# Closing seven-block products: where raw weight chunks lie, how far ahead they are loaded, and where VectorE's sums stand

## The chip, the cores and the metric

The kernel runs on one core of one Trainium2 chip. The metric is device time in microseconds (us), the median of the timed executions. TensorE is called PE, VectorE DVE, ScalarE ACT, GpSimd POOL and SyncE SP, as in the profile; PEld is PE's loading of weights.

## The reference, cut to what matters

An encoder of two layers over 512 tokens of width 1024, in float32. Each layer has an attention part and then a squared-ReLU MLP:

```python
def sq_relu_mlp(h, w_up, w_down):
    u = jax.nn.relu(h @ w_up)
    return (u * u) @ w_down
...
        h = h + sq_relu_mlp(rmsnorm(h, norm_ffn[layer]), ffn_w_up[layer], ffn_w_down[layer])
```

`w_up` is 1024 x 4096 and `w_down` 4096 x 1024. The change concerns a part of `h = h + (u * u) @ w_down` in each of the two layers.

## The kernel before

**Split products.** A float32 product is made of three matmuls: each operand is split into a high half rounded to a shorter format and a low half that holds the rest (high x high, high x low, low x high). For weights, ACT writes the high half (tile `whi`, three buffers) and DVE subtracts it from the raw weights to give the low half (`wlo`, four buffers).

**The down product.** In `mlp` the 32 row blocks of `w_down` are used in three manners: six and, at the end, two (layer 0) or four (layer 1) by plain products, eight by `product8`, and 16 or 14 by `Seven`, a Strassen-like scheme: of a 2 x 2 arrangement of blocks it makes seven products instead of eight, at the price of sums of blocks. I call the `Seven` product of the down matrix the closing product. It has four output blocks m = 0 to 3 (256 columns each), and each takes `np` chunks: 8 in layer 0, 7 in layer 1. So there are 32 and 28 chunks, numbered on from 0 here. A chunk is 21 matmuls of 128x256 on PE (L459 to L461, three for each of seven products).

**A chunk's way** (`seven_chunk`): SP loads two rows of 256 columns (256 KB, L360); three sums of its 128x128 blocks follow (L365, L366, L367), on POOL or, for two chunks (kp 2 and 5) of the output blocks m = 1 to 3, on DVE; ACT makes the high half of all seven blocks in one instruction of 896 columns (L371), DVE the low half (L372). The raw chunk lies in a tile `raw` (four buffers) or in a free slot `a` when more slots are free than `reserve`.

**An output block's end** (`Seven.run` and `evac` in `mlp`): ACT copies one PSUM half (L467), DVE adds the others (L468 to L471) and then adds 128x1024 into `hT` (L1600). `product8` before it ends in eight DVE additions into `hT` (L1556).

**What sets the order.** The program is written in PE's order. `weights(i)` is called for each chunk before its matmuls; it asks for loads up to `LOAD` = 5 chunks ahead, begins the sums of what is loaded, and makes high and low halves two chunks ahead. A scheduler then places each engine's instructions, except where `tc.keep_in_program_order` holds them: POOL's sums are held, DVE's are not. Each engine works its row in order, and SP's queue likewise: an instruction that waits holds what stands behind it.

**Other tiles that the change uses.** `scratch()` gives 128x512 tiles `sc` (six buffers), used for temporary results throughout; `spare_p` gives 128x512 tiles `p` (five buffers), the attention's probability tiles, used in the MLP for the last two operands of `product8`.

Of the kernel before, what the change touches and what calls it, by code (L numbers as in the profile page):

```python
# [8 lines left out]
F32 = mybir.dt.float32  # L9
F32R = mybir.dt.float32r  # L10
I32 = mybir.dt.int32
AF = mybir.ActivationFunctionType
ALU = mybir.AluOpType
# [3 lines left out]
S = 512  # L17
D = 1024
P = 128
# [11 lines left out]
def f32(ap):  # L31
    return ap.bitcast(F32)
# [3 lines left out]
def encoder_kernel(ctx: ExitStack, tc: tile.TileContext, ins, out, dbg=None):  # L36
    nc = tc.nc
    PE, ACT, DVE, POOL, SP = nc.tensor, nc.scalar, nc.vector, nc.gpsimd, nc.sync
# [3 lines left out]
    wp = ctx.enter_context(tc.tile_pool(name="wp", bufs=3))  # L42
# [19 lines left out]
    def nm(s):  # L62
        cnt[0] += 1
        return f"{s}_{cnt[0]}"
# [206 lines left out]
    def rows(w, k0, nk):  # L271
        return w[k0 * P : (k0 + nk) * P, :].rearrange("(k p) n -> p k n", p=P)


    asked, loaded, ready, low_parts = [], [], [], []
    AHEAD, SUM, LOAD = 2, 3, 5
    begun = [0]

    def plan(*spec, make=None, **more):
        asked.append((make or chunk, spec, more))  # L280
        return len(asked) - 1
# [7 lines left out]
    def begin(i):  # L289
        while begun[0] < len(loaded):  # L290
            make = asked[begun[0]][0]
            if make is summed_chunk and begun[0] > i + SUM:
                break
            if make in (summed_chunk, seven_chunk):
                next(loaded[begun[0]])
            begun[0] += 1

    def weights(i, ahead=AHEAD):
        while len(loaded) < min(i + LOAD + 1, len(asked)):
            preload(len(loaded) + 1)  # L300
            begin(i)
        begin(i)
        while len(ready) < min(i + ahead + 1, len(asked)):
            hi, lo, lows = next(loaded[len(ready)])
            ready.append((hi, lo))
            low_parts.append(lows)

            give_low(len(ready) - fixed[0])
        give_low(i + 1)
        return ready[i]  # L310
# [38 lines left out]

    SEVEN = [(0, 0), (2, 2), (4, 5), (3, 3), (5, 4), (6, 1), (1, 6)]

    reserve = [3]
    def seven_chunk(w, k0, c0, eng=None):


        slot = Slot(F32) if len(free) > reserve[0] else None
        raw = slot.t if slot else wp.tile([P, 1024], F32, tag="raw", bufs=4, name=nm("raw"))
        SP.dma_start(raw[:, 0:512].rearrange("p (k n) -> p k n", k=2), rows(w, k0, 2)[:, :, c0 : c0 + 256])  # L360
        r = raw.rearrange("p (b n) -> p b n", n=P)
        yield
        held = (lambda z: z) if eng else tc.keep_in_program_order
        eng = eng or POOL
        held(eng.tensor_tensor(r[:, 6], r[:, 0], r[:, 1], op=ALU.subtract))  # L365
        held(eng.tensor_tensor(r[:, 4:6], r[:, 2:3].to_broadcast([P, 2, P]), r[:, 0:7:6], op=ALU.add))  # L366
        held(eng.tensor_tensor(r[:, 7], r[:, 3], r[:, 5], op=ALU.subtract))  # L367
        yield
        hi = wp.tile([P, WIDE], F32R, tag="whi", name=nm("whi"))[:, 16:912]
        lo = wp.tile([P, WIDE], F32R, tag="wlo", bufs=4, name=nm("wlo"))[:, 48:944]  # L370
        ACT.activation(hi, raw[:, 128:1024], AF.Copy)  # L371
        DVE.tensor_tensor(lo, raw[:, 128:1024], f32(hi), op=ALU.subtract)  # L372
        if slot:
            slot.free()
        yield hi, lo, []

    class Seven:
# [60 lines left out]
            for s_ in self.slots.values():  # L438
                s_.free()

        def plan(self, w, c0, pairs=None):

            return [plan(w, pairs[kp] if pairs else 2 * kp, c0, DVE if pairs and c0 and kp in (2, 5) else None,
                         make=seven_chunk)
                    for kp in range(self.np)]

        def run(self, ids, evac):
# [1079 lines left out]
    def mlp(l, last=None, then=lambda: None):  # L1527

        stage, ahead, later = first_product(l)
        reserve[0] = 3
        w = ins["ffn_w_down"][l]
        up4, gens4 = [], []

        def plain_last(k0, V):
            left = list(V)
            gens4.extend(product(w, k0, up4, tiles(512 * c, 512), lambda j, b, c=c: ev(4 * c + j, b), nk=2 * len(V))
                         for c in range(2))  # L1540

            def beside(m, i):
                if m == 2 and i % 8 == 4 and left:
                    w_ = left.pop(0)
                    for z in range(2):
                        U4.append(Slot())
                        up4.append(U4[-1].pair())
                        split(w_.t[:, S * z : S * z + S], up4[-1])
                    w_.free()

            return beside

        U4 = []

        def ev(m, b):
            return DVE.tensor_tensor(hT[:, m, :], hT[:, m, :], b, op=ALU.add)  # L1556

        U, _, _, (at_u, _), _ = stage(SIZES[l][0])
        up = [s_.pair() for s_ in U]
        gens = [product(w, at_u, up, tiles(512 * c, 512), lambda j, b, c=c: ev(4 * c + j, b)) for c in range(2)]  # L1560
        ahead()
        for c, gen in enumerate(gens):
            for i, _ in enumerate(gen):
                later(c, i)
        for s_ in U:
            s_.free()
        ids8 = []
        U, R, V, (at_u, at_r), late = stage(*SIZES[l][1:], lambda at: ids8.extend(
            plan8(w, [k + z for k in at for z in range(2)])))
        gen = product8(ids8, U, ev)  # L1570
        u7 = Seven(2 * len(R))
        ids = [u7.plan(w, 256 * m, at_r) for m in range(4)]
        k0 = 32 - 2 * len(V)
        beside = (last or plain_last)(k0, V)
        then()
        bias = iter(()) if last else bias_rows()
        reserve[0] = NSLOT
        work, at = convert(u7, R), 0
        for _ in range(10):
            next(work)  # L1580
        for i, _ in enumerate(gen):
            if i in (1, 4, 6):
                next(late, None)
            next(bias, None)

            at += 9 * len(R) + 2
            while at > 0:
                next(work, None)
                at -= 8 * len(U) - 2
        for x in (work, bias):  # L1590
            for _ in x:
                pass
        reserve[0] = 3 if last else 2
        for m in range(4):
            if m == 1 and not last:
                hold["tables"].free()

            def evac(w_):
                h2 = hT[:, 2 * m : 2 * m + 2, :]
                DVE.tensor_tensor(h2, h2, w_.t.rearrange("p (z n) -> p z n", z=2), op=ALU.add)  # L1600

            for i, _ in enumerate(u7.run(ids[m], evac)):
                beside(m, i)
        u7.free()
        for gen in gens4:
            for _ in gen:
                pass
        for s_ in U4:
            s_.free()
# [530 lines left out]
```

## Time and profile before

| | |
|---|---|
| median of 3 timed runs | 1134.73 us (1134.01 to 1135.53) |
| the profiled execution | 1136.11 us, its span 1134.3 us |
| granted TensorE clock | 0.998 over the span |
| closing products | about 486 to 564 us and 1032 to 1101 us |
| ACT making high halves of raw chunks (L371) | 55.2 us in 58 instructions |
| DVE making low halves of raw chunks (L372) | 69.7 us in 58 instructions |

How to read the rows of the profile: a group has line, engine, operation, output<-input by tile, shape and count, then busy time and mean ns, then the idle time before it and what ended that. A row of the timeline has start, duration, engine, line and tiles, and in brackets the idle time before it and what released it. A row of waits says who waited for whom, with total us, times and longest us. A row of windows has the stretch, its length, and busy us with the count of instructions of PE, PEld, DVE, ACT and POOL, then granted clock, DMA share and GB/s.

### The profile page before, as it was taken

How to read it: one execution, taken by the hardware profiler on the slowest of the kernel's cores; microseconds unless marked ns; L12 is line 12 of the kernel's file. 1: busy time of each engine (PE TensorE's matmuls, PEld its weight loads, DVE VectorE, ACT ScalarE, POOL GpSimd, SP SyncE). 2: the span in 40 equal slices, each digit the busy share in tenths (PEclk: the TensorE clock that was granted, in tenths of full speed). 3: DMA queues.
4: the chain of work that ended last, by engine and by line, in shares of the span. 5: the costliest groups of instructions: out<-in, count | busy, mean ns of one | idle time of the engine just before them, and what ended most of it. 6: DMA issues, size and time to landing. Idle time of an engine off the chain costs nothing.

```text
span 1134.3 us, 20502 instructions
## 1 busy us (share of the span) xinstructions
PE 1121.3 (99%) x7348; PEld 1007.5 (89%) x7348; DVE 904.0 (80%) x1571; ACT 667.8 (59%) x1132; POOL 593.3 (52%) x718
## 2 busy tenths in 40 slices
PE   9999999999999999999999999999999999999997
PEld 7787788888899999899998998988889999989996
DVE  7887997978968787979785676667997788798874
ACT  6677785765346668634464555555552676773334
POOL 4366432226788994378522232221287889535640
PEclk9999999999999999999999999999999999999999
DMA  8322442222533334933576574433344223282342
GB/s 241 102 74 77 117 113 70 66 66 75 167 103 91 96 103 121 287 108 103 154 150 166 145 185 125 125 109 123 103 155 132 75 90 99 78 194 69 101 146 75
DMA packets 117237, 135.54 MB, mean 119 GB/s; under 512 B 9859, under 2 KB 98864, under 8 KB 117136
## 3 DMA queue, kind: packets, MB, share of 16 engines
q1 hardware_dynamic: 110736, 119.83, 34.8%
q0 software_dynamic: 6224, 14.31, 6.5%
q8 instruction: 58, 0.95, 0.4%
q14 instruction: 43, 0.35, 0.1%
q10 hardware_dynamic: 176, 0.10, 0.0%
HBM read 112.18 MB, written 6.29 MB: 104 GB/s over the span
## 4 chain that ended last, share of the span: by engine, by line
PE 86%; DVE 5%; issue 4%; POOL 2%; DMA 2%; ACT 1%; SPq 0%; DVEq 0%; POOLq 0%; ACTq 0%
PE mm L618 8%; PE mm L620 8%; PE mm L619 8%; PE mm L461 4%; PE mm L459 4%; PE mm L460 4%; PE s L1143 3%; PE t L461 3%; PE t L459 3%; PE t L460 3%; PE o L1131 3%; PE s L618 2%; PE s L619 2%; PE s L620 2%; PE s L461 2%
## 5 line engine op out<-in xcount | busy, mean ns | idle before, releaser
L618 PE MATMUL mm<-a,whi 128*128 128x512 f32 x428 | 172.7, 404 | 0.1
L372 DVE TENSOR_TENSOR wlo<-a,whi 128x896 fp32r<-128x896 f32 x106 | 135.3, 1282 | 43.8 <-ACT whi L371 43.6
L619 PE MATMUL mm<-a,whi 128*128 128x512 f32 x428 | 167.5, 391 | 0.0
L620 PE MATMUL mm<-a,wlo 128*128 128x512 f32 x428 | 167.2, 392 | 0.0
L371 ACT ACTIVATE whi<-a 128x896 fp32r<-128x896 f32 x106 | 100.9, 952 | 97.3 <-PE s L460 29.0
L226 DVE TENSOR_TENSOR wlo<-raw,whi 128x1024 fp32r<-128x1024 f32 (+3 forms) x94 | 106.8, 1142 | 24.7 <-ACT whi L236 21.8
L236 ACT ACTIVATE whi<-raw 128x1024 fp32r<-128x1024 f32 (+4 forms) x97 | 89.1, 920 | 56.4 <-PE s L619 23.2
L461 PE MATMUL mm<-a,wlo 128*128 128x256 f32 x430 | 119.6, 278 | 0.8 <-DVE wlo L372 0.8
L459 PE MATMUL mm<-a,whi 128*128 128x256 f32 x430 | 118.8, 276 | 0.0
L460 PE MATMUL mm<-a,whi 128*128 128x256 f32 x430 | 118.8, 276 | 0.0
L371 ACT ACTIVATE whi<-raw 128x896 fp32r<-128x896 f32 x58 | 55.2, 956 | 82.7 <-POOL raw L367 22.7
L367 POOL TENSOR_TENSOR a<-a 128x128 f32<-128x128 f32 x104 | 97.8, 940 | 8.2
L366 POOL TENSOR_TENSOR a<-a 128x256 f32<-128x256 f32 x104 | 94.3, 907 | 8.1
L620 PEld LDWEIGHTS mm<-a,wlo 128*128 128x128 f32 x428 | 80.3, 188 | 17.1
L1151 POOL TENSOR_SCALAR p<-p,ti 128x512 f32<-128x512 f32 x64 | 48.0, 750 | 88.6 <-DVE ti L1150 67.8
L618 PEld LDWEIGHTS mm<-a,whi 128*128 128x128 f32 x428 | 80.5, 188 | 15.4 <-issue 0.7
L619 PEld LDWEIGHTS mm<-a,whi 128*128 128x128 f32 x428 | 80.7, 189 | 13.6
L1783 POOL TENSOR_SCALAR p<-p,ti 128x256 f32<-128x256 f32 x64 | 35.6, 567 | 103.4 <-DVE ti L1782 82.4
L459 PE MATMUL t<-a,whi 128*128 128x256 f32 x312 | 86.1, 276 | 0.0
L460 PE MATMUL t<-a,whi 128*128 128x256 f32 x312 | 86.1, 276 | 0.0
L461 PE MATMUL t<-a,wlo 128*128 128x256 f32 x312 | 86.1, 276 | 0.0
L372 DVE TENSOR_TENSOR wlo<-raw,whi 128x896 fp32r<-128x896 f32 x58 | 69.7, 1223 | 19.6 <-ACT whi L371 19.6
(449 smaller groups left out, 3583.1 us busy)
## 6 DMA issues: line engine op xcount, KB each, us to landing
a<-in_ffn_w_up_dram SPq DMA_DIRECT2D x102, 256.0 KB, 2.7
raw<-in_ffn_w_down_dram SPq DMA_DIRECT2D x34, 512.0 KB, 4.3
raw<-in_ffn_w_down_dram SPq DMA_DIRECT2D x56, 256.0 KB, 2.6
raw<-in_od_w_qkv_dram SPq DMA_DIRECT2D x64, 128.0 KB, 3.2
raw<-in_ffn_w_up_dram SPq DMA_DIRECT2D x12, 512.0 KB, 3.8
wlo<-in_ffn_w_down_dram POOLq DMA_DIRECT2D x12, 512.0 KB, 7.5
a<-a SPq DMA_DIRECT2D x17, 256.0 KB, 3.3
bx<-a SPq DMA_DIRECT2D x32, 128.0 KB, 6.1
```

What stands on the lines that cost most here:

```text
L226: z = lambda: (eng or DVE).tensor_tensor(to, src, f32(high), op=ALU.subtract)
L236: ACT.activation(hi[:, 0:m], raw[:, 0:m], AF.Copy)
L366: held(eng.tensor_tensor(r[:, 4:6], r[:, 2:3].to_broadcast([P, 2, P]), r[:, 0:7:6], op=ALU.add))
L367: held(eng.tensor_tensor(r[:, 7], r[:, 3], r[:, 5], op=ALU.subtract))
L371: ACT.activation(hi, raw[:, 128:1024], AF.Copy)
L372: DVE.tensor_tensor(lo, raw[:, 128:1024], f32(hi), op=ALU.subtract)
L459: PE.matmul(o, wh, x[:, 0], start=kp == 0 and n in (0, 1, 3, 5), stop=False, skip_group_check=True)
L460: PE.matmul(o, wh, x[:, 1], start=False, stop=False, skip_group_check=True)
L461: PE.matmul(o, wl, x[:, 0], start=False, stop=kp == self.np - 1, skip_group_check=True)
L618: PE.matmul(o, wh, xh, start=first, stop=False)
L619: PE.matmul(o, wh, xl, start=False, stop=False)
L620: PE.matmul(o, wl, xh, start=False, stop=last)
```

## The change

Three things, all for closing products alone, except that the sums' place within a raw chunk changes for all seven-block chunks (blocks are renumbered in `SEVEN` to match):

1. Of the 32 and 28 chunks, 15 and 11 are loaded into pairs of tiles, either two `sc` or two `p`, by two loads of 128 KB. The first tile holds blocks a0 to a3, the second b0 to b3. Their high and low halves are made in two instructions each, of 384 and 512 columns. The first four chunks and all others stay in `raw` or `a`.
2. `LOAD` is 8 during the closing products, 5 elsewhere.
3. DVE's sums are put off: they are written when PE's chunk is three before theirs, and held in program order.

```diff
-    AHEAD, SUM, LOAD = 2, 3, 5
+    AHEAD, SUM, LOAD = 2, 3, [5]
+    put_off = []
...
             if make in (summed_chunk, seven_chunk):
-                next(loaded[begun[0]])
+                z = next(loaded[begun[0]])
+                if z:
+                    put_off.append((begun[0], z))
             begun[0] += 1
...
     def weights(i, ahead=AHEAD):
-        while len(loaded) < min(i + LOAD + 1, len(asked)):
+        while len(loaded) < min(i + LOAD[0] + 1, len(asked)):
             preload(len(loaded) + 1)
             begin(i)
         begin(i)
+        while put_off and put_off[0][0] <= i + SUM:
+            put_off.pop(0)[1]()
...
-    SEVEN = [(0, 0), (2, 2), (4, 5), (3, 3), (5, 4), (6, 1), (1, 6)]
+    SEVEN = [(0, 0), (4, 2), (6, 5), (5, 3), (1, 4), (2, 1), (3, 6)]
...
-    def seven_chunk(w, k0, c0, eng=None):
-        slot = Slot(F32) if len(free) > reserve[0] else None
-        raw = slot.t if slot else wp.tile([P, 1024], F32, tag="raw", bufs=4, name=nm("raw"))
-        SP.dma_start(raw[:, 0:512].rearrange("p (k n) -> p k n", k=2), rows(w, k0, 2)[:, :, c0 : c0 + 256])
-        r = raw.rearrange("p (b n) -> p b n", n=P)
+    def seven_chunk(w, k0, c0, eng=None, home=None):
+        slot, src = None, rows(w, k0, 2)[:, :, c0 : c0 + 256]
+        if home:
+            parts = [home(F32) for _ in range(2)]
+            for z in range(2):
+                SP.dma_start(parts[z][:, 0:256], src[:, z])
+        else:
+            slot = Slot(F32) if len(free) > reserve[0] else None
+            raw = slot.t if slot else wp.tile([P, 1024], F32, tag="raw", bufs=4, name=nm("raw"))
+            parts = [raw[:, 512 * z : 512 * z + 512] for z in range(2)]
+            SP.dma_start(raw.rearrange("p (k n) -> p k n", k=2)[:, :, 0:256], src)
+        a, b = (t.rearrange("p (b n) -> p b n", n=P) for t in parts)
         yield
-        held = (lambda z: z) if eng else tc.keep_in_program_order
-        eng = eng or POOL
-        held(eng.tensor_tensor(r[:, 6], r[:, 0], r[:, 1], op=ALU.subtract))
-        held(eng.tensor_tensor(r[:, 4:6], r[:, 2:3].to_broadcast([P, 2, P]), r[:, 0:7:6], op=ALU.add))
-        held(eng.tensor_tensor(r[:, 7], r[:, 3], r[:, 5], op=ALU.subtract))
-        yield
+        held = tc.keep_in_program_order
+        later, eng = eng, eng or POOL
+        def sums():
+            held(eng.tensor_tensor(a[:, 2], a[:, 0], a[:, 1], op=ALU.subtract))
+            held(eng.tensor_tensor(b[:, 2:4], b[:, 0:1].to_broadcast([P, 2, P]), a[:, 0:3:2], op=ALU.add))
+            held(eng.tensor_tensor(a[:, 3], b[:, 1], b[:, 3], op=ALU.subtract))
+        if later:
+            yield sums
+        else:
+            sums()
+            yield
...
-        ACT.activation(hi, raw[:, 128:1024], AF.Copy)
-        DVE.tensor_tensor(lo, raw[:, 128:1024], f32(hi), op=ALU.subtract)
+        for to, x in (((0, 384), parts[0][:, P:512]), ((384, 896), parts[1])) if home else (((0, 896), raw[:, P:1024]),):
+            to = slice(*to)
+            ACT.activation(hi[:, to], x, AF.Copy)
+            DVE.tensor_tensor(lo[:, to], x, f32(hi[:, to]), op=ALU.subtract)
...
-        ids = [u7.plan(w, 256 * m, at_r) for m in range(4)]
+        n7, kinds = len(R), dict(R=None, S=scratch, P=spare_p)
+        homes = [kinds["R" if n < 4 else ("RSRSRSR"[n % 7] if last and n > 10 else "RSRPRSRSP"[n % 9])]
+                 for n in range(4 * n7)]
+        ids = [u7.plan(w, 256 * m, at_r, homes[n7 * m : n7 * m + n7]) for m in range(4)]
...
         reserve[0] = 3 if last else 2
+        LOAD[0] = 8
         for m in range(4):
...
+        LOAD[0] = 5
         u7.free()
```

PE's row of instructions is the same in both kernels. On DVE three places matter. The first is the end of `product8` in layer 0, where its eight additions (L1556, in the changed kernel L1577) stand among the first low halves (L372, now L393) of the closing product. Before, with the sums of chunk 13 in tile a_6094:

```order
L1556 TENSOR_TENSOR hT<-hT,t_5415 128x512
L1556 TENSOR_TENSOR hT<-hT,o_5416 128x512
L365 TENSOR_TENSOR a_6094<-a_6094 128x128
L366 TENSOR_TENSOR a_6094<-a_6094 128x256
L1556 TENSOR_TENSOR hT<-hT,mm_5417 128x512
L367 TENSOR_TENSOR a_6094<-a_6094 128x128
L372 TENSOR_TENSOR wlo_5830<-raw_5654,whi_5829 128x896
L1556 TENSOR_TENSOR hT<-hT,mm_5418 128x512
L1556 TENSOR_TENSOR hT<-hT,mm_5419 128x512
L1556 TENSOR_TENSOR hT<-hT,s_5420 128x512
L372 TENSOR_TENSOR wlo_5849<-raw_5716,whi_5848 128x896
```

and now:

```order
L1577 TENSOR_TENSOR hT<-hT,t_5415 128x512
L1577 TENSOR_TENSOR hT<-hT,o_5416 128x512
L1577 TENSOR_TENSOR hT<-hT,mm_5417 128x512
L393 TENSOR_TENSOR wlo_5830<-raw_5654,whi_5829 128x896
L1577 TENSOR_TENSOR hT<-hT,mm_5418 128x512
L1577 TENSOR_TENSOR hT<-hT,mm_5419 128x512
L1577 TENSOR_TENSOR hT<-hT,s_5420 128x512
L393 TENSOR_TENSOR wlo_5870<-raw_5716,whi_5869 128x896
L393 TENSOR_TENSOR wlo_5900<-raw_5765,whi_5899 128x896
```

The three sums have left this place; they now stand behind the low half of chunk 11. The second place is the end of output block 1 in layer 1 on DVE. The low half behind the 1024-wide addition is chunk 17's, and the sums are chunk 19's (raw_12681 before, sc_12676 and sc_12677 now). Before:

```order
L468 TENSOR_TENSOR a_12670<-a_12670,mm_12457 128x2x256
L469 TENSOR_TENSOR a_12670<-a_12670,mm_12458 128x512
L372 TENSOR_TENSOR wlo_12687<-raw_12580,whi_12686 128x896
L470 TENSOR_TENSOR a_12670<-a_12670,mm_12458 128x256
L365 TENSOR_TENSOR raw_12681<-raw_12681 128x128
L471 TENSOR_TENSOR a_12670<-a_12670,s_12459 128x512
L366 TENSOR_TENSOR raw_12681<-raw_12681 128x256
L1600 TENSOR_TENSOR hT<-hT,a_12670 128x1024
L367 TENSOR_TENSOR raw_12681<-raw_12681 128x128
L372 TENSOR_TENSOR wlo_12724<-raw_12610,whi_12723 128x896
```

and now:

```order
L489 TENSOR_TENSOR a_12770<-a_12770,mm_12545 128x2x256
L490 TENSOR_TENSOR a_12770<-a_12770,mm_12546 128x512
L491 TENSOR_TENSOR a_12770<-a_12770,mm_12546 128x256
L393 TENSOR_TENSOR wlo_12789<-raw_12580,whi_12788 128x896
L492 TENSOR_TENSOR a_12770<-a_12770,s_12547 128x512
L1625 TENSOR_TENSOR hT<-hT,a_12770 128x1024
L393 TENSOR_TENSOR wlo_12823<-sc_12609,whi_12822 128x384
L393 TENSOR_TENSOR wlo_12823<-sc_12610,whi_12822 128x512
L379 TENSOR_TENSOR sc_12676<-sc_12676 128x128
L380 TENSOR_TENSOR sc_12677<-sc_12677,sc_12676 128x256
L381 TENSOR_TENSOR sc_12676<-sc_12677 128x128
L393 TENSOR_TENSOR wlo_12860<-raw_12644,whi_12859 128x896
```

The sums have gone from between the additions to behind chunk 17's low half, which is made in two pieces. At the end of block 0 of layer 0 the order of the additions and of the low halves behind them is as before, except that chunk 10's low half comes in two pieces. The third place is SP's queue at the start of layer 1's closing product (chunks 0 to 2 first; a_12227 is chunk 5 before; the loads of the two kernels carry the lines L360 before, and L372 and L367 now). Before:

```order
L360 DMA raw_12012<-in_ffn_w_down_dram 128x2x256
L360 DMA raw_12058<-in_ffn_w_down_dram 128x2x256
L360 DMA raw_12111<-in_ffn_w_down_dram 128x2x256
L360 DMA a_12227<-in_ffn_w_down_dram 128x2x256
L360 DMA raw_12149<-in_ffn_w_down_dram 128x2x256
L360 DMA raw_12161<-in_ffn_w_down_dram 128x2x256
L360 DMA raw_12263<-in_ffn_w_down_dram 128x2x256
L360 DMA raw_12299<-in_ffn_w_down_dram 128x2x256
L360 DMA raw_12329<-in_ffn_w_down_dram 128x2x256
L360 DMA raw_12359<-in_ffn_w_down_dram 128x2x256
```

and now:

```order
L372 DMA raw_12072<-in_ffn_w_down_dram 128x2x256
L372 DMA raw_12118<-in_ffn_w_down_dram 128x2x256
L372 DMA raw_12171<-in_ffn_w_down_dram 128x2x256
L372 DMA a_12294<-in_ffn_w_down_dram 128x2x256
L367 DMA sc_12287<-in_ffn_w_down_dram 128x256
L372 DMA raw_12209<-in_ffn_w_down_dram 128x2x256
L367 DMA sc_12288<-in_ffn_w_down_dram 128x256
L367 DMA sc_12299<-in_ffn_w_down_dram 128x256
L367 DMA sc_12300<-in_ffn_w_down_dram 128x256
L367 DMA sc_12377<-in_ffn_w_down_dram 128x256
L367 DMA sc_12378<-in_ffn_w_down_dram 128x256
L372 DMA raw_12221<-in_ffn_w_down_dram 128x2x256
```

Chunks 5, 7 and 10 (the sc tiles) and 6 (a_12294) now stand ahead of chunk 4's load into a raw buffer (raw_12221), where loads into raw buffers stood.

More of the change, by code (lines that the diff above doesn't have):

```diff
@@ L439, in free, with plan @@
                 s_.free()
-        def plan(self, w, c0, pairs=None):
+        def plan(self, w, c0, pairs=None, homes=None):
             return [plan(w, pairs[kp] if pairs else 2 * kp, c0, DVE if pairs and c0 and kp in (2, 5) else None,
-                         make=seven_chunk)
+                         make=seven_chunk, home=homes[kp] if homes else None)
                     for kp in range(self.np)]
```

## The prediction, made before the changed kernel ran

> **What bounds the kernel now.** I read the page first, then what TensorE (PE) waits for, then the order of time around each wait.
>
> ```profile
> PE 1121.3 (99%) x7348; PEld 1007.5 (89%) x7348; DVE 904.0 (80%) x1571; ACT 667.8 (59%) x1132; POOL 593.3 (52%) x718
> ...
> PE s L461 <- DVE wlo L372: 1.7, 1, 1.7
> PE mm L461 <- DVE wlo L372: 0.8, 1, 0.8
> ```
>
> PE is busy 99% of the span, so a change that leaves its work alone can win only what PE waits. Its two waits for the low halves of seven-block weights (L372) both lie in the closing products. The page counts a pipelined matmul as busy to its modelled end, so I price a stall from start to start:
>
> ```profile
> 491.55 0.28 PE L460 MATMUL s<-a,whi 128*128 128x256 f32 x1
> 491.84 0.39 PE L461 MATMUL s<-a,wlo 128*128 128x256 f32 x1
> 492.06 0.28 PE L459 MATMUL t<-a,whi 128*128 128x256 f32 x1
> ...
> 513.16 0.28 PE L459 MATMUL mm<-a,whi 128*128 128x256 f32 x1
> 513.27 0.28 PE L460 MATMUL mm<-a,whi 128*128 128x256 f32 x1
> 514.30 0.39 PE L461 MATMUL mm<-a,wlo 128*128 128x256 f32 x1 [0.75 <-DVE wlo L372]
> 514.52 0.28 PE L459 MATMUL mm<-a,whi 128*128 128x256 f32 x1
> ...
> 1073.03 0.28 PE L460 MATMUL s<-a,whi 128*128 128x256 f32 x1
> 1074.96 0.39 PE L461 MATMUL s<-a,wlo 128*128 128x256 f32 x1 [1.65 <-DVE wlo L372]
> 1075.18 0.28 PE L459 MATMUL t<-a,whi 128*128 128x256 f32 x1
> ```
>
> These are the records on both sides of the three places where PE's rhythm breaks. The rhythm itself, from the windows (PE busy first, then PEld, DVE, ACT, POOL; some matmul records are missing, so I count from the code):
>
> ```profile
> 392.00:420.00 28.00, 28.00 (x245) 27.75 (x244) 23.56 (x28) 18.68 (x23) 26.36 (x31) 1.00 0.31 95
> 505.69:525.76 20.07, 19.32 (x170) 19.12 (x169) 16.89 (x20) 8.92 (x11) 17.46 (x20) 1.00 0.37 118
> 525.76:544.80 19.04, 19.04 (x170) 19.04 (x169) 17.10 (x19) 8.98 (x11) 17.44 (x19) 1.00 0.26 85
> ```
>
> The third row is block 2 of layer 0 (blocks and chunks count from 0), eight chunks of 21 matmuls: 19.04 us, so 0.113 a matmul and 2.38 a chunk. The second row holds the second place and as much work: 20.07. Two steps should take 0.23 us; the three places take 0.51, 1.25 and 2.15. That makes stalls of **0.28, 1.02 and 1.92 us, together 3.22**.
>
> **The change, stall by stall.** PE's instruction order is the same row for row, and the new SEVEN numbering only renames blocks, so PE's own work is unchanged: 0. What moves is when low halves are ready. I follow VectorE (DVE) before each stall, in order of time, with ACT's and POOL's groups where they matter.
>
> ```profile
> 485.74 0.77 DVE L365 TENSOR_TENSOR a<-a 128x128 f32<-128x128 f32 x1 [1.58 <-DMA a<-in_ffn_w_down_dram]
> 486.54 0.65 DVE L366 TENSOR_TENSOR a<-a 128x256 f32<-128x256 f32 x1
> ...
> 487.71 0.28 DVE L367 TENSOR_TENSOR a<-a 128x128 f32<-128x128 f32 x1
> ...
> 490.70 3.35 DVE L372 TENSOR_TENSOR wlo<-raw,whi 128x896 fp32r<-128x896 f32 x3
> ```
>
> Stall 1 (0.28): DVE stood 1.58 us for the load of chunk 13, then spent 0.77+0.65+0.28 = 1.7 on its sums, amid the evacuations (L1556), and chunk 2's low half (first of the three from 490.70), for which PE stood at 491.55, came after that. The change moves these sums some thirty rows back. Up to 3.3 us comes free ahead of a 0.28 us miss. Gain 0.28.
>
> ```profile
> 506.55 1.25 DVE L372 TENSOR_TENSOR wlo<-raw,whi 128x896 fp32r<-128x896 f32 x1 [1.34 <-ACT whi L371]
> 507.73 0.68 DVE L468 TENSOR_TENSOR a<-a,t 128x512 f32<-128x512 f32 x1
> ...
> 511.49 1.49 DVE L1600 TENSOR_TENSOR hT<-hT,a 128x1024 f32<-128x1024 f32 x1
> 512.90 2.61 DVE L372 TENSOR_TENSOR wlo<-raw,whi 128x896 fp32r<-128x896 f32 x2
> ...
> L371 ACT ACTIVATE whi<-raw 128x896 fp32r<-128x896 f32 x58 | 55.2, 956 | 82.7 <-POOL raw L367 22.7
> ...
> POOL raw L365 <- DMA raw<-in_ffn_w_down_dram: 7.3, 3, 4.8
> ```
>
> Stall 2 (1.02): the burst that adds block 0 into hT (L468 to L1600) started at 507.73, because chunk 9's low half held DVE to 507.80; chunk 11's low half, the first of the two from 512.90, came behind the burst. Chunk 9 was late because ScalarE (ACT) waits for GpSimd's (POOL's) sums more than for anything else ahead of raw chunks, and POOL had stood 4.8 us for a load: four raw buffers, none free. Now chunk 5 lies in scratch tiles, so that wait need not stand there and POOL gains some 4 us of lead. Chunk 9 is then held only by its whi buffer (three of them), which PE gives back after chunk 6. Chunk 11 starts at 513.16, so chunk 7 starts at 513.16 - 4 x 2.38 = 503.64; 0.96 for the high half and 1.23 for the low half later it is 505.8. The burst starts at 506.0 to 506.4, after block 0's end at 506.0, some 1.3 us earlier or more, against a miss of 1.02. The margin is thin. Gain 1.02, bounds 0 to 1.02.
>
> ```profile
> 1067.15 1.08 DVE L372 TENSOR_TENSOR wlo<-raw,whi 128x896 fp32r<-128x896 f32 x1
> ...
> 1069.84 0.82 DVE L365 TENSOR_TENSOR raw<-raw 128x128 f32<-128x128 f32 x1 [1.28 <-DMA raw<-in_ffn_w_down_dram]
> 1070.59 0.67 DVE L471 TENSOR_TENSOR a<-a,s 128x512 f32<-128x512 f32 x1
> 1071.18 0.58 DVE L366 TENSOR_TENSOR raw<-raw 128x256 f32<-128x256 f32 x1
> 1071.69 1.76 DVE L1600 TENSOR_TENSOR hT<-hT,a 128x1024 f32<-128x1024 f32 x1
> 1073.37 0.54 DVE L367 TENSOR_TENSOR raw<-raw 128x128 f32<-128x128 f32 x1
> ```
>
> Stall 3 (1.92): sums of chunk 19 stand inside the burst; DVE waited 1.28 us for their load and spent 0.82+0.58+0.54 = 1.94 on them. Pinned, they follow chunk 17's low half. That frees 3.2 us ahead of a 1.92 us miss. Gain 1.92.
>
> **What it adds.** 26 chunks (15 and 11) lie in pairs of tiles, so their split takes two instructions on ACT and on DVE, and their load two issues.
>
> ```profile
> L372 DVE TENSOR_TENSOR wlo<-raw,whi 128x896 fp32r<-128x896 f32 x30 | 36.3, 1227 | 10.8 <-ACT whi L371 10.8
> L468 DVE TENSOR_TENSOR a<-a,t 128x512 f32<-128x512 f32 x8 | 5.4, 676 | 0.0
> L470 DVE TENSOR_TENSOR a<-a,t 128x256 f32<-128x256 f32 x8 | 3.3, 409 | 0.0
> ...
> raw<-in_ffn_w_down_dram SPq DMA_DIRECT2D x56, 256.0 KB, 2.6
> raw<-in_od_w_qkv_dram SPq DMA_DIRECT2D x64, 128.0 KB, 3.2
> ```
>
> From 256 to 512 columns a DVE instruction grows from 409 to 676 ns, 1.04 ns a column, which leaves 0.14 us that each instruction costs anyway. 26 x 0.14 = 3.6 us of DVE, at most five in a block, 0.7 us there: 17.10 busy of 19.04 becomes 17.8, still inside. ACT pays alike and is busy under 9 of 19. Its cover is the lead; with that gone, 0.14 us falls on PE at a block's critical chunk. I take 0, bounds 0 to 0.7. Half loads bound at 2.6 to 3.2 us to landing; eight chunks ahead is 8 x 2.38 = 19 us, so 0. New waits for scratch or probability tiles: bounds 0 to 1.92 each (the third stall, the nearest wait of this kind); by the plan a tile's next chunk comes seven to twelve after the one it holds, so it is free about when its load is asked for; I take 0. Left over I allow 0.1.
>
> POOL's sums show what DVE does to them:
>
> ```profile
> 508.63 0.75 POOL L366 TENSOR_TENSOR raw<-raw 128x256 f32<-128x256 f32 x1
> 509.46 1.19 POOL L367 TENSOR_TENSOR raw<-raw 128x128 f32<-128x128 f32 x1
> 1070.59 0.46 POOL L367 TENSOR_TENSOR raw<-raw 128x128 f32<-128x128 f32 x1
> ```
>
> The same L367 takes 0.46 us, or 1.19 where DVE's 1.22 us L372 runs beside it. [...]
>
> **Sum.** Against the profiled execution (1136.11 us; its span of 1134.3 and 1.8 around it): 1136.1 - 3.2 + 0.1 = 1133.0. That execution was 1.4 over the median; from the median, 1134.73 - 3.1 = **1131.6 us**. About 0.2% (2.3 us) is what a measurement of this kernel can tell from no change.
>
> **The rivals.**
> - *The burst stays late.* In both blocks the low half behind the burst keeps its place behind the 1024-wide add. If DVE reaches the burst over 0.3 us later than I work out, stall 2 stays in part or whole, and the longer splits push the same way in stall 3. Keeping 1.02 gives 1132.5, keeping 1.92 gives 1133.4. For: the thin margin, DVE at 17 of 19 us. Against: block 2 of layer 0 passes already, with a burst that has three sums in it. Chance 0.20.
> - *No lead.* Loads are asked for eight ahead but the tiles aren't free, and POOL waits as before; only stall 1 goes: 1134.4. Against: SyncE's new order has scratch loads right behind the first raw ones. Chance 0.10.
> - *Pinned sums wait: slower.* DVE works in order, and twelve chunks' sums are now held in program order ahead of a low half. If a load lands after DVE gets there, everything behind stands, as in stall 3, at 1.92 each. Over 0.2% slower needs 3.2 + 2.3 = 5.5 us, three such waits: 1131.5 + 3 x 1.92 = 1137.3. It decides where SyncE issues that load less than about 3 us before DVE arrives. For: SyncE's queue is in order, and a load that waits for its tile holds those behind it. Against: the 19 us. Chance 0.06.
> - *The pair as bound.* [...] Chance 0.02.
>
> **How the numbers follow.** All three stalls gone: 0.62, at 1131.6 with 0.7 either way, the spread of the runs before. Nothing can come out below but this spread: low 1130.8. The range takes in the late burst and most of no lead: high 1134.2. Faster is the first case, 0.62; within 0.2% the second and third, 0.30; slower the last two, 0.08.
>
> **What would show it.** Right: no PE wait for the low half in either closing product, blocks of 19.04 and 16.66 us throughout, no DVE idle time ahead of its own sums for a load, POOL's 4.8 us wait gone, hT's burst starting within a microsecond of the block's end. Wrong: a block longer than 19.04, with a wait for the low half behind the 1024-wide add (late burst) or for a load ahead of DVE's sums (pinned sums); and any loss outside the two closing products, in the transitions that use the same scratch and probability tiles.

## The result and the profile after

The changed kernel takes **1146.4 us** (median; 1144.26 to 1146.89) beside 1135.53 for the kernel before in the same comparison: ratio 1.0085, 95% interval 1.0075 to 1.0096. It is slower by some ten microseconds, where 3.1 were to be won. Its profiled execution took 1146.45 us with a span of 1144.7, 10.4 more than before.

The first line is from its page, the others are from the waits of TensorE:

```profile
PE 1125.7 (98%) x7348; PEld 1010.5 (88%) x7348; DVE 914.6 (80%) x1597; ACT 669.9 (59%) x1158; POOL 586.0 (51%) x718
PE s L639 <- ACT whi L268: 7.0, 1, 7.0
PE s L482 <- DVE wlo L393: 1.6, 2, 1.4
...
PE mm L482 <- DVE wlo L393: 0.2, 1, 0.2
```

PE's waits for low halves (L393, before L372) sum to 1.8 us, where 2.5 were. But a new wait stands above them: 7.0 us, once, for a high half that L268 writes. That is not a line of the closing products. It belongs to `product8`, the stage ahead of them. PE's order of time there:

```profile
476.45 0.39 PE L640 MATMUL s<-p,whi 128*128 128x512 f32 x1
476.68 0.39 PE L641 MATMUL s<-p,wlo 128*128 128x512 f32 x1
484.04 0.80 PE L639 MATMUL s<-p,whi 128*128 128x512 f32 x1 [6.97 <-ACT whi L268]
484.63 0.63 PE L640 MATMUL s<-p,whi 128*128 128x512 f32 x1
485.05 0.63 PE L641 MATMUL s<-p,wlo 128*128 128x512 f32 x1
...
489.75 0.46 PE L640 MATMUL t<-p,whi 128*128 128x512 f32 x1
490.04 0.39 PE L641 MATMUL t<-p,wlo 128*128 128x512 f32 x1
490.27 0.39 PE L639 MATMUL o<-p,whi 128*128 128x512 f32 x1
```

From 476.68 to 484.04 are 7.36 us where one step of 0.23 was due: a stall of 7.13. Behind it the same matmuls go 0.43 us apart instead of 0.23 until 490.04. The windows show why in the column after POOL's count, the granted clock, 0.64 and 0.51 in the second and third rows:

```profile
472.00:478.00 6.00, 5.07 (x23) 3.86 (x21) 0.00 (x0) 0.00 (x0) 1.25 (x3) 1.00 1.06 299
478.00:484.00 6.00, 0.00 (x0) 0.00 (x0) 2.91 (x4) 2.73 (x4) 4.21 (x6) 0.64 0.30 97
484.00:490.00 6.00, 5.96 (x14) 4.76 (x15) 5.80 (x11) 2.40 (x4) 2.78 (x3) 0.51 0.61 195
490.00:496.00 6.00, 6.00 (x28) 4.92 (x28) 5.96 (x12) 1.58 (x3) 0.00 (x0) 1.00 0.43 139
```

Fourteen matmuls from 484.04 to 490.04 took 6.00 us instead of 14 x 0.227 = 3.18, so 2.82 more. Stall and slow clock make 9.95 of the 10.4 us.

Who kept ACT? First its order of time in the changed kernel, then the same place before:

```profile
480.43 0.63 ACT L1000 ACTIVATE a<-a 128x512 fp32r<-128x512 f32 x1 [12.40 <-DMA bx<-a]
480.96 0.61 ACT L447 ACTIVATE a<-sc 128x512 fp32r<-128x512 f32 x1
482.41 0.63 ACT L447 ACTIVATE a<-a 128x512 fp32r<-128x512 f32 x1 [0.83 <-DVE a L452]
482.94 1.04 ACT L268 ACTIVATE whi<-raw 128x1024 fp32r<-128x1024 f32 x1
```

```profile
469.72 0.63 ACT L426 ACTIVATE a<-a 128x512 fp32r<-128x512 f32 x1 [1.22 <-DVE a L431]
470.30 1.07 ACT L268 ACTIVATE whi<-raw 128x1024 fp32r<-128x1024 f32 x1
471.27 0.61 ACT L426 ACTIVATE a<-a 128x512 fp32r<-128x512 f32 x1
```

Before, L268 ran at 470.30. Now an instruction that wasn't there, L1000, stands ahead of it and waits 12.40 us for transfers `bx`, and ACT works its row in order: L268 starts at 482.94. DVE, which subtracts L1000's result, stood as well:

```profile
481.09 0.69 DVE L997 TENSOR_TENSOR a<-a,a 128x512 fp32r<-128x512 f32 x1 [11.38 <-ACT a L1000]
```

L1000 (L979 before) makes the high half of the activations for the two last row blocks of layer 0; I call it, with its low half L997 (L976), **the V split**. `beside` in `plain_last` writes it into the program in output block 2 of the closing product. In ACT's row (its instructions in order, counted in the program) it stood there before, behind the high half of chunk 17 (row 500, L979). Now its first half is row 472:

```
469 L268 ACTIVATE whi_5665<-raw_5458 128x1024
470 L447 ACTIVATE a_5576<-a_4867 128x2x256
471 L263 ACTIVATE wlo_5656<-raw_5537 128x1024
472 L1000 ACTIVATE a_6419<-a_5388 128x512
473 L447 ACTIVATE a_5625<-sc_5613 128x2x256
474 L447 ACTIVATE a_5626<-a_4999 128x2x256
```

**Theory.** A free slot is taken from the head of a list. Followed through the program (no trace shows which slot a tile lies in), the list holds slots 8 and 0 when the V split asks for its two in the kernel before, so the first half goes into 8, which a chunk had just used, and slot 0 had held block 1's sum. With pairs fewer chunks take a slot, and the list reads 0, 8, 14: the first half of the V split goes into slot 0. That slot held the tables of the bias (`hold["tables"]`), whose last readers are the `bx` transfers. Nothing else in the program stood between them and L1000 any more, so the scheduler placed it 28 rows earlier, where the transfers had not ended. **Rival:** SP's queue, with twice the issues for pairs and eight chunks of loads, delays `bx`, and ACT would have waited in any place.

### The profile page after: what moved, and what is told of

Its sections match the earlier page's. It is cut to its first block, busy times and chain, and to the rows that moved or that the text cites. A ratio compares the mean times of both kernels' runs of the same rounds, so it can differ in the third digit from the quotient of the medians.

```text
span 1144.7 us, 20639 instructions
## 1 busy us (share of the span) xinstructions
PE 1125.7 (98%) x7348; PEld 1010.5 (88%) x7348; DVE 914.6 (80%) x1597; ACT 669.9 (59%) x1158; POOL 586.0 (51%) x718
## 4 chain that ended last, share of the span: by engine, by line
PE 79%; DVE 6%; issue 6%; DMA 3%; ACT 2%; POOL 2%; SPq 0%; POOLq 0%; DVEq 0%; ACTq 0%
PE mm L639 8%; PE mm L641 8%; PE mm L640 8%; PE mm L482 3%; PE mm L480 3%; PE mm L481 3%; PE s L1164 3%; PE o L1152 3%; PE t L482 2%; PE s L639 2%; PE t L480 2%; PE t L481 2%; PE s L640 2%; DVE wlo L393 2%; PE t L1139 2%
## 5 line engine op out<-in xcount | busy, mean ns | idle before, releaser
L393 DVE TENSOR_TENSOR wlo<-a,whi 128x896 fp32r<-128x896 f32 x104 | 135.1, 1304 | 43.3 <-ACT whi L392 43.0
L381 POOL TENSOR_TENSOR a<-a 128x128 f32<-128x128 f32 x103 | 102.7, 997 | 8.1
L641 PEld LDWEIGHTS mm<-a,wlo 128*128 128x128 f32 x428 | 80.3, 188 | 17.1
L380 POOL TENSOR_TENSOR a<-a 128x256 f32<-128x256 f32 x103 | 90.0, 873 | 8.1
L639 PEld LDWEIGHTS mm<-a,whi 128*128 128x128 f32 x428 | 80.5, 188 | 15.4 <-issue 0.7
L640 PEld LDWEIGHTS mm<-a,whi 128*128 128x128 f32 x428 | 80.7, 189 | 13.6
L482 PEld LDWEIGHTS mm<-a,wlo 128*128 128x128 f32 x430 | 80.7, 188 | 1.3 <-DVE wlo L393 0.8
L481 PEld LDWEIGHTS mm<-a,whi 128*128 128x128 f32 x430 | 80.7, 188 | 0.1
```

The costliest lines, as they stand in the source:

```text
L380: held(eng.tensor_tensor(b[:, 2:4], b[:, 0:1].to_broadcast([P, 2, P]), a[:, 0:3:2], op=ALU.add))
L381: held(eng.tensor_tensor(a[:, 3], b[:, 1], b[:, 3], op=ALU.subtract))
L393: DVE.tensor_tensor(lo[:, to], x, f32(hi[:, to]), op=ALU.subtract)
L481: PE.matmul(o, wh, x[:, 1], start=False, stop=False, skip_group_check=True)
L482: PE.matmul(o, wl, x[:, 0], start=False, stop=kp == self.np - 1, skip_group_check=True)
L639: PE.matmul(o, wh, xh, start=first, stop=False)
```

## The experiments

Each kernel was timed beside the kernel before, and each ratio is to that. They are called e1 to e4 and e6 to e13, as in the expectations; "repaired" is e3. The diffs are against the changed kernel, except e2's, which is against the kernel before. Lines of code inserted shift the line numbers below them by one to three.

**e1: another slot.** One line in `beside` ahead of the two slots:

```diff
+                    free.append(free.pop(0))
                     for z in range(2):
                         U4.append(Slot())
```

> The changed kernel, but the first half of the plain product's operand takes another free slot than the one that held the bias tables. Theory (slot): ScalarE's high half of that operand was placed ahead of product8's last high half because its slot seemed free, and waited 12.4 us for the loads of bx to have read the tables; TensorE stood 7.1 us and then ran 14 matmuls at half clock, 2.8 us. With another slot it stands late in ScalarE's row, no wait, no throttled stretch: about 10 us come back, 1136 us or less beside 1146 for the changed kernel. If the two small new stalls (0.5 and 1.7 us in layer 0) are late effects of the same wait they go too: 1133. Rival (SyncE's queue): the new scratch loads hold up SyncE and with it the loads of bx; then a slot changes nothing: 1146.

1136.98 us, ratio 1.0001 (0.999 to 1.0012). The wait for L268 is gone.

**e2: the kernel before with the tables' slot given to the V split.**

```diff
+                    hold["tables"].free()
+                    free.insert(0, free.pop())
                     for z in range(2):
...
-            if m == 1 and not last:
-                hold["tables"].free()
```

> The kernel before, with nothing of the change, but the tables are given back only when the plain product's operand is split, and its first half takes their slot. ScalarE's row then has that high half ahead of product8's last one, as in the changed kernel. Theory (slot): the wait for bx, the stall and the throttled stretch come with it: about 10 us more than before, 1145. Rival (SyncE's queue): no new loads, so no loss: 1135.

1151.69 us, ratio 1.0133 (1.0119 to 1.0148): more than expected. Its waits of PE:

```profile
PE s L618 <- ACT whi L268: 6.8, 1, 6.8
PE mm L461 <- DVE wlo L372: 4.0, 2, 3.7
```

The first is the wait of the changed kernel, made with no pairs, no loads eight ahead and no late sums. At the end of `product8` PE has fallen 8.85 us behind. The second row is another event, 5.6 us in block 3: sums that are not held stand there inside the adds into hT and wait 1.92 us for their load, as in the third stall of before. PE stalls for 3.8 us, and 3.41 us at half the clock follow.

**e3: the V split held in its place** (the repaired kernel).

```diff
-                        split(w_.t[:, S * z : S * z + S], up4[-1])
+                        src, d = w_.t[:, S * z : S * z + S], up4[-1]
+                        tc.keep_in_program_order(ACT.activation(d[:, 0, :], src, AF.Copy))
+                        tc.keep_in_program_order(DVE.tensor_tensor(d[:, 1, :], src, f32(d[:, 0, :]), op=ALU.subtract))
```

> The changed kernel with the same slots, but the two instructions of the plain product's operand are held in program order, so they can't move ahead. Theory (slot): the slot does harm only through ScalarE's order: the same as with the other slot, within 0.1%. Rival: writing into the tables' slot costs by itself: still some us slower.

1136.79 us, ratio 1.0002 (0.9993 to 1.0011). Here the slot is the same as in the changed kernel, and only the place differs. So slot, place and loss belong together. SP's queue is out as a cause: it has as many issues in e1 and e3, without the loss, and those of the kernel before in e2, with it.

**e4: repaired, without pairs** (`homes` all `None`).

> As the one with the split held, and without the pairs of tiles: every closing chunk in raw buffers or free slots; loads eight ahead and VectorE's sums late and pinned stay. Theory: the late sums alone take away the first and third stall of before (0.28 and 1.92), the second (1.02) needs the extra buffers: 1.0 us slower than with the pairs, about 2 us under before. Rival: with four raw buffers the pinned sums wait for their loads in VectorE's row and stall as before or worse: 1135 or more.

1136.66 us, ratio 0.9999 (0.9987 to 1.0011). So with its accident mended the change wins nothing that can be measured, with pairs or without. The rest of the work asked where the 3.1 us went.

To see that, I put each kernel's matmuls beside the same matmuls of before (their order is the same in all) and noted by how much PE falls back (+) or gains (-) in each stretch of the profiled execution. Times in the head are those of before; "elsewhere" is work outside the stretches that the edits aim at, and shows how far one execution differs from another.

| kernel | 473-487: end of product8 | 487-529: blocks 0, 1 | 529-540: into block 2 | 540-556: to block 3 | 1036-1127: layer 1 | elsewhere |
|---|---|---|---|---|---|---|
| forecast | 0 | -1.30 | 0 | 0 | -1.92 | 0 |
| after | +9.99 | -0.85 | +1.89 | 0.00 | -1.53 | +0.91 |
| e1 other slot | 0.00 | -0.64 | +2.71 | 0.00 | -1.55 | +0.36 |
| e2 before, slot given | +8.85 | -0.68 | +0.87 | +5.59 | -1.21 | +0.04 |
| e3 repaired | 0.00 | -1.18 | +2.69 | 0.00 | -1.31 | -0.21 |
| e4 no pairs | 0.00 | -1.19 | +2.82 | +0.92 | -1.87 | +1.44 |
| e6 sums beside loads | 0.00 | +0.93 | +1.51 | +1.17 | +0.01 | +0.46 |
| e7 late in layer 1 | 0.00 | +6.09 | +1.07 | +0.68 | -1.52 | +1.18 |
| e8 before, late in layer 1 | 0.00 | +0.07 | 0.00 | +0.08 | -0.68 | -1.34 |
| e9 before, late in both | 0.00 | -0.52 | +1.07 | 0.00 | -0.88 | -0.19 |
| e10 sums six ahead | 0.00 | -1.37 | +1.19 | +0.69 | -1.38 | +1.47 |
| e11 and V split later | 0.00 | -0.32 | +0.35 | +1.93 | -1.40 | +0.01 |
| e12 V split later alone | 0.00 | +0.62 | +0.92 | +1.10 | -1.53 | +0.46 |
| e13 as e11, no pairs | 0.00 | +0.26 | 0.00 | +2.68 | -0.31 | +1.60 |

Each row of the table is one execution, and kernels with the same rows of instructions tell how much that is worth. e1 and e3 have the same rows on every engine and differ by 0.5 us in blocks 0, 1. e6 and e7 (below) have the same rows in layer 0 and lose 0.93 and 6.09 there. The kernel before and e2 have the same rows in layer 1, with the sums inside the adds, and yet e2 is 1.21 us faster. There its sums wait 0.56 us for their load, where before they waited 1.28, and the third stall is 0.5 us instead of 1.92:

```profile
1083.91 0.79 DVE L365 TENSOR_TENSOR raw<-raw 128x128 f32<-128x128 f32 x1 [0.56 <-DMA raw<-in_ffn_w_down_dram]
```

So a difference of about a microsecond in one cell shows no cause by itself.

The gains came in the second and fifth columns. The third gives them back: 2.7 us in the repaired kernel. PE's waits there, then DVE's and ACT's rows:

```profile
532.18 0.39 PE L482 MATMUL s<-a,wlo 128*128 128x256 f32 x1 [0.27 <-DVE wlo L393]
...
533.32 0.39 PE L482 MATMUL t<-a,wlo 128*128 128x256 f32 x1 [0.52 <-DVE wlo L393]
...
539.07 0.39 PE L482 MATMUL s<-a,wlo 128*128 128x256 f32 x1 [0.71 <-DVE wlo L393]
```

```profile
529.92 1.48 DVE L1627 TENSOR_TENSOR hT<-hT,a 128x1024 f32<-128x1024 f32 x1
531.32 1.95 DVE L393 TENSOR_TENSOR wlo<-sc,whi 128x384 fp32r<-128x384 f32 x2
533.19 0.94 DVE L1571 TENSOR_TENSOR a<-a,a 128x512 fp32r<-128x512 f32 x1
534.05 0.54 DVE L379 TENSOR_TENSOR p<-p 128x128 f32<-128x128 f32 x1
534.52 1.08 DVE L393 TENSOR_TENSOR wlo<-raw,whi 128x896 fp32r<-128x896 f32 x1
535.52 0.95 DVE L380 TENSOR_TENSOR p<-p,p 128x256 f32<-128x256 f32 x1
536.51 0.43 DVE L381 TENSOR_TENSOR p<-p 128x128 f32<-128x128 f32 x1
537.31 1.70 DVE L393 TENSOR_TENSOR wlo<-p,whi 128x512 fp32r<-128x512 f32 x2 [0.37 <-ACT whi L392]
```

```profile
536.65 1.05 ACT L392 ACTIVATE whi<-p 128x512 fp32r<-128x512 f32 x2 [3.69 <-DVE p L380]
```

DVE has no idle time from the 1024-wide add to 536.94. In this stretch stand chunk 19's low half in two pieces, a half of the V split, and the three sums of chunk 21, for which ACT then waits 3.69 us. PE waits 0.71 us for chunk 21's low half, until 539.07. Before, the sums of the same chunk ran at 521, in block 1, ahead of the adds:

```profile
521.20 0.51 DVE L365 TENSOR_TENSOR a<-a 128x128 f32<-128x128 f32 x1 [0.23 <-DMA a<-in_ffn_w_down_dram]
```

**Theory:** "three chunks ahead" puts this chunk's sums into the fullest place of DVE. **Rivals:** the pieces and the eight loads ahead cost it.

**e6 and e7: sums not put off**, in both layers (e6) or in layer 0 only (e7); the rest as repaired.

```diff
-        if later:
+        if later and LATE[0]:
             yield sums
```

This is cut from e7's edit: `LATE[0]` is `bool(last)`, and DVE's sums are not held where it is false. e6 does the same in both layers, without the flag.

> The repaired kernel (V split held in program order) with DVE's sums neither put off nor pinned, so that they stand where the kernel before has them: beside the loads; pairs and eight loads ahead stay. Theory 'late sums fill the burst': in the repaired kernel PE lost 2.8 us in layer 0 in chunks 12 to 20, because chunk 21's sums, which before ran at 521 us, now stand at 534 us between the adds into hT, the second V split and the low halves. So these stalls should shrink below 1 us here, while the 1.9 us stall of layer 1 may come back where a sum stands in front of a load again; time 2 us under to 1 us over the kernel before. Rival 'pairs': the split in two pieces and the loads ahead cost the 2.8 us, so they stay and the time is 1 to 3 us over.

> The repaired kernel with DVE's sums put off and pinned in layer 1 only; in layer 0 as in e6. Theory 'late sums fill the burst': layer 0 loses nothing any more between 514 and 541 us and keeps what it won (0.3 and 0.9), layer 1 keeps its 1.9: 2.5 to 3.1 us under the kernel before (ratio 0.9973 to 0.998). Rival 'pairs': as the repaired kernel, within 0.5 us of the kernel before.

1142.13 us, ratio 1.0044 (1.0028 to 1.0059), and 1141.48, ratio 1.0038 (1.0023 to 1.0052): slower by five microseconds and more, against theory and rivals alike. The column "into block 2" did shrink (2.69 to 1.51 and 1.07), but blocks 0 and 1 lost, by very different amounts in the two executions. DVE and PE in e7, where the lines are L380 to L382 for sums and L394 for a low half:

```profile
490.73 0.75 DVE L380 TENSOR_TENSOR a<-a 128x128 f32<-128x128 f32 x1 [1.84 <-DMA a<-in_ffn_w_down_dram]
491.40 0.68 DVE L1580 TENSOR_TENSOR hT<-hT,mm 128x512 f32<-128x512 f32 x1
492.00 0.56 DVE L381 TENSOR_TENSOR a<-a 128x256 f32<-128x256 f32 x1
492.60 0.69 DVE L382 TENSOR_TENSOR a<-a 128x128 f32<-128x128 f32 x1
493.21 1.08 DVE L394 TENSOR_TENSOR wlo<-raw,whi 128x896 fp32r<-128x896 f32 x1
```

```profile
494.35 0.58 PE L483 MATMUL s<-a,wlo 128*128 128x256 f32 x1 [4.36 <-DVE wlo L394]
```

With loads asked for eight ahead, sums beside the loads stand at the end of `product8`, wait for transfers and hold the low halves behind them: the first stall of before, with a wait of 4.36 us where 0.28 were lost (1.58 us in e6). So putting the sums off is what makes eight loads ahead bearable, and its distance is wrong for chunk 21.

**e8 and e9: the kernel before with late, held sums alone**, in layer 1 (e8) or in both (e9): `homes` all `None`, `LOAD` 5, V split held.

> The kernel before with one thing of the change: DVE's sums late and pinned, in layer 1 alone (no pairs, five loads ahead; the V split held, too). Theory 'the place of the sums is all that matters': the 1.9 us stall of layer 1 goes, the 0.28 and 1.02 us stalls of layer 0 stay: 1.9 us under the kernel before (ratio 0.9983). Rival 'the lead from pairs and loads ahead won it': the stall stays, no change.

> As e8, with the sums late and pinned in both layers. Theory 'late sums fill the burst': layer 0 loses 2 to 3.8 us in chunks 17 to 20 with raw buffers and five loads ahead as well, so 1.5 to 3.5 us over e8, about the kernel before or 1 us more. Rival 'pairs' or 'loads ahead': no such loss, layer 0's first stall (0.28) gone, 0 to 0.5 us under e8.

1136.34 us, ratio 0.9994 (0.9985 to 1.0003), and 1135.92, ratio 0.9992 (0.9983 to 1.0). e8 comes out between theory and rival; e9's time is 0.4 us under e8's, as its rivals had it. Neither can be told from the kernel before by the 0.2% that a measurement shows with safety. In the table both win in layer 1 (-0.68, -0.88), but e2 wins as much there with its sums unmoved, so what the sums' place is worth in layer 1 isn't shown. In layer 0, e9, with neither pairs nor more loads ahead, loses 1.07 us into block 2, where DVE makes chunk 21's sums at 532.51 to 536.12 and PE waits for that chunk; e8, with these sums in their old place, loses nothing. I put so much of the repaired kernel's 2.69 down to chunk 21's sums. The other 1.6 came with pairs or loads ahead. Experiment e4, without pairs, loses 3.7 us into block 2 and to block 3, some 1.6 of that by a half clock (last section), so the loads ahead may have a part in it; pairs and loads weren't taken apart further.

**e10: sums six chunks ahead**; the rest as repaired.

```diff
-        while put_off and put_off[0][0] <= i + SUM:
+        while put_off and put_off[0][0] <= i + 6:
```

> The repaired kernel (V split held, pairs, eight loads ahead) with DVE's sums written six chunks ahead of theirs instead of three, still held in program order. All sums then stand in the middle of a block, away from the adds into hT. Theory 'late sums fill the burst': of the 2.8 us that the repaired kernel lost in chunks 17 to 21 of layer 0, the 1.0 that chunk 21 waits for its own sums goes and most of the rest; what stays is the V split in the burst. Layer 1 keeps its 1.9. 1.5 to 3 us under the kernel before (ratio 0.9974 to 0.9987). Rival 'six ahead is too early': sums stand for their load as in the two runs with sums not put off, 1.7 to 4.5 us at the end of product8; then slower than before.

1135.71 us, ratio **0.9988 (0.9979 to 0.9997)**, about 1.4 us (0.0012 x 1136.75) under the kernel before and the best of all, though that is less than 0.2%. The sums now stand away from the adds into hT in both layers; the loss into block 2 falls from 2.69 to 1.19, and of the three PE waits there one is left, on chunk 19's low half:

```profile
533.73 0.39 PE L482 MATMUL t<-a,wlo 128*128 128x256 f32 x1 [0.53 <-DVE wlo L393]
```

With pairs, six ahead isn't too early.

**e11 and e12: the V split moved behind the adds**, from `i % 8 == 4` to `i == 30` in block 2, with sums six (e11) or three ahead (e12).

> As e10, with the V split (two ACT and two DVE instructions) moved from PE's chunk 16 to chunk 20, behind the adds into hT. Theory 'the burst is overfull': no PE wait for a low half is left in layer 0; all of the forecast gain, 3.1 us under the kernel before (ratio 0.9973). Rival 'the burst was never the cause': as e10.

> The repaired kernel (sums three ahead) with only the V split moved behind the burst. Theory 'the burst is overfull': DVE has 2.1 us less in it, so the 2.8 us lost in chunks 17 to 21 shrink to under 1; 1.5 to 3 us under the kernel before. Rival 'the place of chunk 21's sums alone': chunk 21 still waits about 1 us, 1 to 2 us under.

1137.72 us, ratio 1.0007 (0.9998 to 1.0016), and 1137.28, ratio 1.0005 (0.9996 to 1.0015). The loss into block 2 shrinks as expected (1.19 to 0.35, 2.69 to 0.92) but comes back one block later (0.69 to 1.93, 0 to 1.10), and the second stall is back. Both kernels are slower than e10, by 2.0 and 1.6 us of median. So the theory seems to hold only for the place: moved, the same DVE work may be late elsewhere. But the edit has a side effect (below), so this isn't shown. How full DVE is, by windows of the kernel before, the repaired one and e10:

```profile
525.00:545.00 20.00, 20.00 (x179) 20.00 (x178) 18.06 (x19) 9.08 (x12) 18.32 (x20) 1.00 0.28 92
```

```profile
525.00:545.00 20.00, 18.50 (x156) 17.73 (x155) 19.10 (x23) 8.43 (x15) 18.90 (x23) 1.00 0.20 61
```

```profile
525.00:545.00 20.00, 19.47 (x165) 18.90 (x165) 19.76 (x24) 9.20 (x15) 18.90 (x22) 1.00 0.20 60
```

The third of the five busy times is DVE: 18.06, 19.10, 19.76 of 20 us. An instruction's busy time can be far above the shortest of its form (POOL's L367 takes 0.46 to 1.40 us in the closing products of the kernel before), but in the last two there is hardly any idle room left to move something into.

The second stall stands ahead of the V split's new place as of its old one, so the split's DVE work can't have brought it back. What differs is seen on POOL's sums of chunk 4 behind `product8`, first in e10, then in e11:

```profile
487.92 0.78 POOL L379 TENSOR_TENSOR raw<-raw 128x128 f32<-128x128 f32 x1 [2.89 <-DMA raw<-in_ffn_w_down_dram]
```

```profile
489.01 0.47 POOL L379 TENSOR_TENSOR raw<-raw 128x128 f32<-128x128 f32 x1 [3.96 <-DMA raw<-in_ffn_w_down_dram]
```

From there the profile marks no idle time of POOL before chunk 11 in either, so a load that lands 1.1 us later shifts the sums and high halves behind it by up to that much. Why it lands later is seen on SP. In e11 its queue has a load more here than in e10, into a free slot, and the load waits (the first line is from SP's waits, the others are from its order of time):

```profile
SPq L372 <- DMA bx<-a: 1.3, 4, 0.4
...
479.23 0.38 SPq L372 DMA_DIRECT2D a<-in_ffn_w_down_dram  x1
479.71 0.41 SPq L372 DMA_DIRECT2D raw<-in_ffn_w_down_dram  x1
```

It is the accident of the changed kernel once more. With the V split later, chunk 27 lies in a free slot instead of a raw buffer (its sums run at 537.46 on POOL). The load at 479.23 waits for the last readers of the tables' slot, `bx`, so it goes into that slot, some 50 us ahead of the place where the program asks for it. The raw load behind it goes out at 479.71; in e10 it follows the one before directly and is issued by 478.59. e12 has the same wait (1.3 us). So e11 and e12 moved the V split and hit this, too, and how much of their time each made isn't known. That the later load brought the second stall back is argued, not shown: in e4 POOL waits 4.06 us for chunk 5, and the stall is gone.

**e13: as e11, without pairs.**

> As e11 without pairs: all chunks in raw buffers and slots, eight loads asked for ahead, sums written six ahead, V split behind the burst. Theory 'pairs give the lead': there aren't the buffers for loads six ahead, so sums stand for their loads and stalls come back, 1 to 4 us over e11. Rival 'pairs do nothing': as e11.

1140.05 us, ratio 1.0024 (1.0012 to 1.0036), 2.3 us over e11, as the theory has it: without the pairs' buffers DVE's sums stand for their loads, 2.32 and 1.30 us in layer 0 and up to 2.94 us in layer 1, where e11 has no such wait.

## Why the prediction was wrong

- **The step that failed:** "PE's instruction order is the same row for row … so PE's own work is unchanged: 0. What moves is when low halves are ready." The sum had no term for rows of other engines that the change moves without touching them. Pairs take fewer slots from the list, another instruction gets another slot, and the scheduler moves it ahead of the high half that PE needs at the end of `product8`. Shown by e1, e2 and e3; worth 9.99 of 10.4 us in the profile. The list of what would show the prediction wrong did name a loss in the transitions, but put it to scratch and probability tiles, and no rival had it as a mechanism.
- **The range** (up to 1134.2) took in the late burst and most of no lead, and nothing from outside the closing products.
- **Stalls 1 and 2 (1.30):** right in the changed kernel to 0.85 and in the repaired to 1.18. The margin of the second is as thin as written: it is back in e11 and e12. That POOL's wait for a load set it isn't borne out, nor that it takes the scratch tiles to end it: e4, without pairs, wins 1.19 with a wait of 4.06 us, where before had 4.83, and with chunk 9's sums beginning at 502.46 on POOL, where they began at 502.66. In the repaired kernel the wait was 2.75 us, not nothing.
- **Stall 3 (1.92):** gone in the changed kernel, with a gain of 1.3 to 1.5 over layer 1 in the changed and the repaired one. But the price was read from one execution. In e2 the same rows in the same order lost 0.5 there, so up to 1.4 of the 1.92 may have been that execution's late load, and what the sums' new place wins is open.
- **What it adds (0, bounds 0 to 0.7, "still inside"):** mis-sized. Into block 2 of layer 0 it cost 1.89 in the changed kernel and 2.69 in the repaired one. The pieces were counted by an estimated 0.14 us each, and the late sums counted only as moved, "some thirty rows back", never for where they land. Chunk 21's land in the fullest place of DVE, 1.07 us by e9.
- **The rival "pinned sums wait":** that it had the sign right is luck, the mechanism was another. In the changed and the repaired kernel no sum on DVE in the closing products waited as long as 0.3 us for its load; unpinned ones did (PE waited 4.36 us in e7), and pinned ones waited long only in e13, without pairs and six ahead (up to 2.94 us).
- **The rival "the pair as bound":** its chance of 0.02 is part of the 0.08 for slower. Its condition, DVE and POOL strictly in turn, is shown by no run. In the window of the repaired kernel above DVE is busy for 19.10 and POOL for 18.90 of 20 us, and at the shortest time that each form takes in this trace, POOL's instructions and those of DVE that don't read PSUM add up to 23.2 us (an estimate), more than the 20.

## What to carry to other kernels

Where tiles come from a shared list, a change of who takes one changes where others land, and a scheduler may then move an instruction across a stage: compare the rows of every engine over the whole program, and price each row that moved ahead of something PE waits for. An engine that is 90% busy in a stretch (DVE before, 18.06 of 20 us) has little place for work "put off": follow each moved instruction to where it lands and count what stands behind it there. Hold an instruction in program order where its early place can only do harm. Price a stall from more than one execution before counting on its gain.

## What the runs showed of the hardware

- **A long wait cost more than itself.** By the clock records of the traces, PE's granted clock was 0.5 for 10.24 us at the 7.13 us stall of the changed kernel (5.8 of them behind its end), and for 6.83 at the 4.52 us stall of e7. That is three and two times the 3.41 us of e2 and e4, within 0.02. In the changed kernel the clock was halved at 479.64, 2.57 us after the last matmul's end at 477.07.
- **Half clock also followed short waits close together.** In e4 stalls of 0.75 and 1.11 us, ending 1.4 us apart, were followed by half clock, 3.41 us in the records:

```profile
537.00:541.00 4.00, 2.47 (x19) 2.08 (x18) 2.85 (x3) 2.63 (x3) 3.74 (x5) 0.99 0.04 10
541.00:545.00 4.00, 4.00 (x24) 4.00 (x23) 2.48 (x3) 0.95 (x1) 3.84 (x5) 0.58 0.38 125
```

  No idle gap of PE was longer than 0.94 us there, so this stretch had no long gap ahead of it. A single stall of 1.75 us in e6 had no such stretch behind it (the mean granted clock of that execution was 0.998, as before; e4's was 0.996). What sets off a stretch of half clock isn't shown.
